# Layer 0's gate and second-norm modulations handed out by the list of stages

## The chip, the cores and the metric

The kernel runs on one core of a Trainium2 chip. The metric is the device time of one execution, in microseconds (us). The engines are TensorE (PE, with its weight loads shown as PEld), VectorE (DVE), ScalarE (ACT), GpSimd (POOL) and SyncE (SP), whose queue issues the DMAs.

## What is computed

A decoder trunk of two layers, over 256 tokens of width 1024, in float32. Cut to what bears on the change:

```python
cond = jax.nn.silu(c)
for l in range(DEPTH):
    mod = cond @ ada_w[l] + ada_b[l]
    sh1, sc1, g1, sh2, sc2, g2 = jnp.split(mod, 6, axis=-1)
    h = rms_norm(x, norm1_g[l]) * (1.0 + sc1) + sh1
    proj = h @ w_in[l]                      # z, xbc, dt, mq, mk, mv, sq, sk, sv
    y = concat(ssd(z, xbc, dt), moba(mq, mk, mv), swa(sq, sk, sv)) @ w_out[l]
    x = x + g1 * y
    h = rms_norm(x, norm2_g[l]) * (1.0 + sc2) + sh2
    x = x + g2 * peer_ffn(h)
```

The six modulations of a layer are vectors of 1024. Here `sh1` and `sc1` are numbers 0 and 1, the gate `g1` is number 2, `sh2` and `sc2` are 3 and 4.

## The kernel before

**One step of a modulation.** A modulation is computed in 8 pieces of 128 channels. One piece is one step: a DMA of 128x1025 floats (512.5 KB, L204, tile `adaw`) and one VectorE instruction that multiplies it by the conditioning row and adds it up into a column of `modc` (L192). `ada_ahead` makes the steps as closures: step i issues the load of piece i+3 and then the VectorE instruction of piece i. In layer 0 the `adaw` tiles are four buffers of the pool `mix0` (tags oH and oL, two each), so a load waits until the instruction on the piece four before it has ended. The same buffers are used at the end of the mixers for the last split of `w_out`.

**Layer 0 has 40 steps before its mixers end.** The first 16 (`early`, modulations 0 and 1) are needed for the first norm: `norm_h` makes `acol` (L264) from them and then h (L284 on VectorE, L282 on ScalarE), two blocks of channels at a time, in four rounds (the loop over `FIRST`). The other 24 (`late`: gate, second shift, second scale) stand in the list `todo`. Their results are read by `gate_row` (L312, the gate) and by the `norm_h` ahead of PEER (modulations 3 and 4), both at the end of the mixers.

**Who takes steps from the list.** `later()` pops steps, two per call (RATE is 2.0). It is called through `tick[0]` each time a chunk of input weights is fetched (in `units`, `proj_parts_whole` and `proj_tokens_whole`), from the stage `rest` on, and four times in the loop over `w_out`. Counted in the code: 8 steps are handed out in `rest` (4 chunks), 2 in `ss`, 4 in `c2`, 4 in `z0`, 4 in `c3` and the last 2 in `z1`.

**Order.** The stages of the mixers follow the string `ORDER[l]`; for layer 0: rest (values and dt), c0 and c1 (convolutions), mv (MoBA's values), ss (sliding-window scores), mp, seg (the decays), c2, z0 (gate z), sv, c3, tok, stb, z1, cb, st, sp. This is the order in which instructions are written down. The kernel is built with `schedule_with_timeline_sim=True`: a planner then chooses the order on each engine by its own estimate of times, and an instruction written earlier goes first among those it takes to be ready. Each engine executes its instructions in the order so chosen. `tc.issue_after(ins)` makes the instructions in its block that are on the engine of `ins` stand behind `ins`.

**dt's chain** is in `values_dt`: L612 adds the bias to dt, L617 to L628 compute softplus on VectorE with two ScalarE activations (L620, L626), and L631 makes `a`, which the decays need (`segr` on GpSimd L642, cumulated sums on TensorE L636, L637, L644).

**Weights.** Projections of the mixers take 512 KB chunks: ScalarE rounds (L173, tile `wH`), and in layer 0 GpSimd makes the remainder in two halves (L176, tile `wL`; `low_of` is "h"). The first projections in layer 0 use the chunks as they are (L360, L375). `wH` and `wL` have three buffers each.

Of the kernel before, what the change touches and what calls it, by code (L numbers as in the profile page):

```python
# [17 lines left out]
ALU = mybir.AluOpType  # L18
# [4 lines left out]
P = 128  # L23
D = 1024
S = 256
NC = 2
# [13 lines left out]
NCAND = 80  # L40
GH = 4
RB = 5
RATE = 2.0
PT = (0, 0)
CV = (1, 0)
WHOLE0 = "mq mk sq xbc0 xbc1"
# [2 lines left out]
    (("- - - mq", "mq"), ("mk mk - sq sq", "mq mk sq"), ("mq - mk -", "mq mk"), ("sq sq", "mq mk sq")),  # L49
)  # L50
ORDER = (
    "rest c0 c1 mv ss mp seg c2 z0 sv c3 tok stb z1 cb st sp",
    "rest c0 mv c1 mp seg ss c2 z0 sv c3 tok stb z1 cb st sp",
)
low_of = ["h"]
# [35 lines left out]
def trunk(ctx: ExitStack, tc: tile.TileContext, x_in, c_in, ada, cols, rows, w_in, w_out, wq, keysT, uT, vT, fg, out, dbg=None):  # L91
    nc = tc.nc
    V, A, G, T = nc.vector, nc.scalar, nc.gpsimd, nc.tensor
# [3 lines left out]
    st = ctx.enter_context(tc.tile_pool(name="st", bufs=2))  # L97
# [218 lines left out]
    tick = [lambda: None]  # L316
# [74 lines left out]
    def mixers(l, xp, mx, xt, xn, modc, colt, early, late):  # L391
        if True:
            def new(shape, tag, dt=F32, bufs=1):
                return mx.tile(shape, dt, tag=tag, name=tag, bufs=bufs)
# [122 lines left out]
                    put_y(self.yn, self.blk0, 2)  # L517

            todo = list(late)
            due = [0.0]  # L520

            def later():
                due[0] += RATE
                while todo and due[0] >= 1.0:
                    due[0] -= 1.0
                    todo.pop(0)()

            xbcT = new([P, 8, S], "xbcT")

# [17 lines left out]
            def gate_z(q):  # L547
                for c, pc in enumerate(proj_tokens(wl, *off[f"z{q}"])):
                    A.activation(sz[c][:, q * 256:(q + 1) * 256], pc[:, :256], AF.Silu)
# [18 lines left out]
            for p, names in enumerate(FIRST[l]):  # L568
# [3 lines left out]
                ada = early[4 * p:4 * p + 4]  # L572
# [10 lines left out]
                        halves.pop(0)()  # L583
            for g in part.values():
                assert next(g, None) is None
            tick[0] = later
            if l == 0:
                proj_tokens_rest = lambda: proj_tokens_whole(wl, *off["rest"], whole)
            else:
# [14 lines left out]
            dt = new([P, NC, 8], "dt")  # L604
            a = new([P, NC, 8], "a")
# [3 lines left out]
            def values_dt():  # L609

                for c, pc in enumerate(proj_tokens_rest()):
                    V.tensor_tensor(out=dtp[:, c, :], in0=pc[:, 0:8], in1=rowt[:, 0:8], op=ALU.add)  # L612
                    A.copy(vx[:, c, :, 0:64], pc[:, 8:392].rearrange("p (h d) -> p h d", d=64))


                na = new([P, NC, 8], "na")
                V.tensor_scalar(out=na, in0=dtp, scalar1=-1.0, scalar2=None, op0=ALU.mult)  # L617
                V.tensor_tensor(out=na, in0=na, in1=dtp, op=ALU.min)
                ey = new([P, NC, 8], "ey")
                A.activation(ey, na, AF.Exp)  # L620
                e1 = new([P, NC, 8], "e1")
                V.tensor_scalar(out=e1, in0=ey, scalar1=1.0, scalar2=None, op0=ALU.add)
                er = new([P, NC, 8], "er")
                V.tensor_scalar(out=er, in0=e1, scalar1=1.0, scalar2=None, op0=ALU.subtract)
                V.tensor_tensor(out=er, in0=ey, in1=er, op=ALU.subtract)
                A.activation(e1, e1, AF.Ln)  # L626
                V.tensor_tensor(out=er, in0=er, in1=e1, op=ALU.add)
                V.scalar_tensor_tensor(out=dt, in0=dtp, scalar=0.0, in1=er, op0=ALU.max, op1=ALU.add)  # L628
                ah = new([P, 8], "ah")
                A.activation(ah, rowt[:, 8:16], AF.Exp)  # L630
                V.scalar_tensor_tensor(out=a, in0=dt, scalar=-1.0, in1=ah[:, None, :].to_broadcast([P, NC, 8]), op0=ALU.mult, op1=ALU.mult)  # L631

            def decays():

# [55 lines left out]
            def swa_scores():  # L690
# [9 lines left out]

            stages = {
                "rest": values_dt, "ss": swa_scores, "mv": moba.values, "mp": moba.put,
                "sv": lambda: att["s"].values(), "sp": lambda: att["s"].put(),
                "c0": lambda: conv(0), "c1": lambda: conv(1), "c2": lambda: conv(2), "c3": lambda: conv(3),
                "z0": lambda: gate_z(0), "z1": lambda: gate_z(1),
                "seg": decays, "tok": tokens, "stb": state_in, "cb": scores_cb, "st": state,
            }
            for name in ORDER[l].split():
                stages[name]()
# [32 lines left out]
            for n in range(2):  # L742
                for q in range(2):
                    h, lo = split(fetch(w_out[l, n, 1, :, q * 1024:(q + 1) * 1024]), LOWM(q))
                    later()
                    for c in range(NC):
                        out_mm(c, n, 1, q, h, lo)
                if n == 0:
                    ssd_out(1)
                put_chunk(n, ysn[n], 4)  # L750
# [294 lines left out]
    for l in range(DEPTH):  # L1045
        own = lambda i: mx.tile([P, D + 1], F32, tag="oL" if i % 2 else "oH", name="adaw", bufs=2)
        adas = ada_ahead([(0, (0, 1), mod[0])] + [(0, (m,), mod[0]) for m in (2, 3, 4)], own, conds[mx]) if l == 0 else []
        h_open(l)
        low_of[0] = "v" if l else "h"
        mixers(l, xp, mx, xt, xn, *mod, adas[:2 * KD], adas[2 * KD:])  # L1050
        if dbg:
            dbg(f"x_mid{l}", xt)
# [108 lines left out]
```

## Time and profile before

| | |
|---|---|
| Time, median of 3 runs | 1942.69 us (1938.9 to 1942.85) |
| The profiled execution's own time | 1945.66 us |
| Its span, first to last instruction | 1943.9 us |
| TensorE busy, share of the span | 1879.8 us, 97% |
| VectorE busy | 1403.6 us, 72% |
| Mean granted TensorE clock | 0.983 |

The mixers of layer 0 fill the first 176 us of the span; there the new x is written out and PEER begins. Times in the rows are us from the start of the span; a bracket at the end of a row of the timeline is how long the engine had been idle and what released it.

### The profile page before, as it was taken

How to read it: one execution, taken by the hardware profiler on the slowest of the kernel's cores; microseconds unless marked ns; L12 is line 12 of the kernel's file. 1: busy time of each engine (PE TensorE's matmuls, PEld its weight loads, DVE VectorE, ACT ScalarE, POOL GpSimd, SP SyncE). 2: the span in 40 equal slices, each digit the busy share in tenths (PEclk: the TensorE clock that was granted, in tenths of full speed). 3: DMA queues.
4: the chain of work that ended last, by engine and by line, in shares of the span. 5: the costliest groups of instructions: out<-in, count | busy, mean ns of one | idle time of the engine just before them, and what ended most of it. 6: DMA issues, size and time to landing. Idle time of an engine off the chain costs nothing. (4 is left out here: it accounts for less than half of the span.)

```text
span 1943.9 us, 33211 instructions
## 1 busy us (share of the span) xinstructions
PE 1879.8 (97%) x12714; PEld 1707.9 (88%) x12714; DVE 1403.6 (72%) x2686; ACT 939.6 (48%) x1473; POOL 420.2 (22%) x255
## 2 busy tenths in 40 slices
PE   7798999999999999999989899999999999999998
PEld 5577999999999888888878789999999998888886
DVE  5955897889963898966657659968899346666665
ACT  2453545544444544545537444455444444555554
POOL 1263789100014001000001147960000320000000
PEclk8889999999999999999999999999999999999999
DMA  9833455444455999865543344554444555665563
GB/s 351 323 126 123 163 167 189 165 158 155 161 165 183 373 357 346 319 205 195 194 129 113 128 148 161 186 184 153 162 154 162 175 184 194 224 196 194 192 194 118
DMA packets 103984, 377.55 MB, mean 194 GB/s; under 512 B 12049, under 2 KB 12305, under 8 KB 103313
## 3 DMA queue, kind: packets, MB, share of 16 engines
q1 hardware_dynamic: 103824, 375.43, 57.1%
q8 instruction: 99, 1.62, 0.4%
q14 instruction: 61, 0.49, 0.1%
HBM read 372.24 MB, written 3.15 MB: 193 GB/s over the span
## 5 line engine op out<-in xcount | busy, mean ns | idle before, releaser
L173 ACT CAST wH<-raw 128x1024 fp32r<-128x1024 f32 x577 | 602.6, 1045 | 517.2 <-PE pu L181 349.1
L176 DVE TENSOR_TENSOR wL<-raw,wH 128x1024 fp32r<-128x1024 f32 (+1 forms) x435 | 532.9, 1226 | 215.7 <-ACT wH L173 214.7
L180 PE MATMUL pu<-hH,wH 128*128 128x256 f32 x2048 | 581.1, 284 | 6.0 <-ACT act L791 6.0
L182 PE MATMUL pu<-hH,wL 128*128 128x256 f32 x2048 | 575.7, 281 | 0.0
L181 PE MATMUL pu<-hL,wH 128*128 128x256 f32 x2048 | 575.3, 281 | 0.0
L176 POOL TENSOR_TENSOR wL<-raw,wH 128x1024 fp32r<-128x1024 f32 (+1 forms) x178 | 365.2, 2071 | 641.0 <-ACT wH L173 620.9
L181 PE MATMUL pacc<-wL,aH 128*128 128x512 f32 x1008 | 393.3, 390 | 0.0
L180 PEld LDWEIGHTS pu<-hH,wH 128*128 128x128 f32 x2048 | 386.4, 189 | 6.8 <-ACT act L791 6.8
L182 PE MATMUL pacc<-wH,aL 128*128 128x512 f32 x1008 | 392.4, 389 | 0.0
L181 PEld LDWEIGHTS pu<-hL,wH 128*128 128x128 f32 x2048 | 386.9, 189 | 0.0
L182 PEld LDWEIGHTS pu<-hH,wL 128*128 128x128 f32 x2048 | 386.6, 189 | 0.0
L180 PE MATMUL pacc<-wH,aH 128*128 128x512 f32 x1008 | 272.5, 389 | 0.0
L999 ACT CAST aH<-act 128x256 fp32r<-128x256 f32 x256 | 103.5, 407 | 323.5 <-PE pacc L181 323.5
L180 PEld LDWEIGHTS pacc<-wH,aH 128*128 128x128 f32 x1008 | 189.3, 188 | 39.5
L182 PEld LDWEIGHTS pacc<-wH,aL 128*128 128x128 f32 x1008 | 189.3, 188 | 39.1
L181 PEld LDWEIGHTS pacc<-wL,aH 128*128 128x128 f32 x1008 | 189.3, 188 | 38.9
L1000 DVE TENSOR_TENSOR aL<-act,aH 128x256 fp32r<-128x256 f32 x256 | 108.2, 425 | 100.1 <-ACT aH L999 99.8
L192 DVE SCALAR_TENSOR_TENSOR adaw<-adaw,crow 128x1025 f32<-128x1025 f32 x96 | 120.5, 1261 | 17.2 <-DMA adaw<-in_ada_dram 17.1
L1089 POOL TENSOR_TENSOR x<-x,fgb 128x512 f32<-128x512 f32 x2 | 2.6, 1293 | 350.0 <-ACT junk L232 350.0
L960 DVE SCALAR_TENSOR_TENSOR act<-pc,act 128x160 f32<-128x160 f32 (+30 forms) x126 | 38.5, 306 | 44.6 <-PE pc L954 44.6
L236 POOL TENSOR_TENSOR hr<-hm,mhalf 128x1 f32<-128x1 f32 x10 | 6.6, 664 | 285.8 <-DVE hm L234 285.8
L946 DVE TENSOR_TENSOR o<-iotax,idx 128x1024 f16<-128x1024 f16 x64 | 47.0, 735 | 17.2 <-ACT idx L915 17.1
(425 smaller groups left out, 2430.9 us busy)
## 6 DMA issues: line engine op xcount, KB each, us to landing
raw<-in_uT_dram SPq DMA_DIRECT2D x256, 512.0 KB, 3.6
raw<-in_vT_dram SPq DMA_DIRECT2D x256, 512.0 KB, 4.4
adaw<-in_ada_dram SPq DMA_DIRECT2D x96, 512.5 KB, 6.0
raw<-in_w_in_dram SPq DMA_DIRECT2D x33, 512.0 KB, 5.4
raw<-in_wq_dram SPq DMA_DIRECT2D x32, 512.0 KB, 3.6
raw<-in_w_out_dram SPq DMA_DIRECT2D x16, 512.0 KB, 3.6
whole<-in_w_in_dram SPq DMA_DIRECT2D x5, 512.0 KB, 10.5
raw<-in_w_in_dram SPq DMA_DIRECT2D x6, 392.0 KB, 3.1
```

The costliest lines, as they stand in the source:

```text
L173: A.copy(h[:, :n], src)
L176: eng.tensor_tensor(out=lo[:, o:o + step], in0=src[:, o:o + step], in1=h[:, o:o + step].bitcast(F32), op=ALU.subtract)
L180: T.matmul(o, l[0], r[0], start=start, stop=False)
L181: T.matmul(o, l[0], r[1], start=False, stop=False)
L182: T.matmul(o, l[1], r[0], start=False, stop=stop)
L192: V.scalar_tensor_tensor(out=src, in0=src, scalar=1.0, in1=cond, op0=ALU.mult, op1=ALU.mult, accum_out=modc[:, m, k:k + 1])
L236: pin[0] = G.tensor_tensor(out=r, in0=ms, in1=mhalf, op=ALU.pow).ins
L946: V.tensor_tensor(out=o1, in0=io, in1=view(idx1), op=ALU.is_equal)
L960: V.scalar_tensor_tensor(out=a, in0=pv[:, lo:hi, :], scalar=1.0 / WSCALE, in1=a, op0=ALU.mult, op1=ALU.mult)
L999: A.copy(aH, act)
L1000: V.tensor_tensor(out=aL, in0=act, in1=aH.bitcast(F32), op=ALU.subtract)
L1089: (V if c else G).tensor_tensor(out=xt[:, c, cs], in0=xt[:, c, cs], in1=fgb[:, cs], op=ALU.mult)
```

## The change

The rate and the tick are gone. `later()` now takes two steps per call and is a stage of its own, `ada`, which stands eight times in layer 0's list, first behind `seg`: 16 steps there, and 8 in the loop over `w_out`, 24 in all as before. All VectorE instructions of these steps are put behind `step`, the instruction at L631 that ends dt's chain. The loads are issued by SP and are not put behind it. In layer 1 the list is empty before and after.

```diff
-RATE = 2.0
 ORDER = (
-    "rest c0 c1 mv ss mp seg c2 z0 sv c3 tok stb z1 cb st sp",
+    "rest c0 c1 mv ss mp seg ada c2 ada ada z0 ada ada sv c3 ada ada tok stb z1 ada cb st sp",
     "rest c0 mv c1 mp seg ss c2 z0 sv c3 tok stb z1 cb st sp",
 )
...
             todo = list(late)
-            due = [0.0]
-
-            def later():
-                due[0] += RATE
-                while todo and due[0] >= 1.0:
-                    due[0] -= 1.0
-                    todo.pop(0)()
+            step_ins = []
+
+            def later(n=2):
+
+                with tc.issue_after(step_ins[0]) if step_ins else nullcontext():
+                    for _ in range(n):
+                        if todo:
+                            todo.pop(0)()
...
             for g in part.values():
                 assert next(g, None) is None
-            tick[0] = later
...
-                V.scalar_tensor_tensor(out=a, in0=dt, scalar=-1.0, in1=ah[:, None, :].to_broadcast([P, NC, 8]), op0=ALU.mult, op1=ALU.mult)
+                step = V.scalar_tensor_tensor(out=a, in0=dt, scalar=-1.0, in1=ah[:, None, :].to_broadcast([P, NC, 8]), op0=ALU.mult, op1=ALU.mult)
+                step_ins.append(step.ins)
...
-                "seg": decays, "tok": tokens, "stb": state_in, "cb": scores_cb, "st": state,
+                "ada": later, "seg": decays, "tok": tokens, "stb": state_in, "cb": scores_cb, "st": state,
```

## Rows read from the trace of the kernel before

**Rows 1.** The page: busy tenths and clock in 40 slices of the span

```profile
PE   7798999999999999999989899999999999999998
PEclk8889999999999999999999999999999999999999
```

**Rows 2.** Stretches: length; busy us of PE, PEld, DVE, ACT, POOL; clock; DMA share; GB/s

```profile
85.20:107.20 22.00, 13.55 (x65) 9.81 (x64) 21.09 (x41) 7.64 (x20) 7.17 (x5) 0.70 0.63 213
107.20:140.00 32.80, 31.79 (x247) 29.82 (x247) 12.83 (x31) 16.55 (x29) 22.92 (x20) 0.99 0.34 113
...
104.00:108.00 4.00, 4.00 (x21) 3.90 (x21) 3.41 (x6) 0.60 (x1) 1.70 (x1) 0.54 0.02 4
```

**Rows 3.** The same for the instructions on adaw alone: busy us of DVE, clock, DMA

```profile
85.20:107.20 22.00, 14.38 (x20) 0.70 0.63 213
```

**Rows 4.** Timeline of VectorE, 47 to 52 us: start, us, line, operation

```profile
47.73 0.16 DVE L264 SCALAR_TENSOR_TENSOR acol<-modc,colt 128x2 f32<-128x2 f32 x1
47.81 1.22 DVE L192 SCALAR_TENSOR_TENSOR adaw<-adaw,crow 128x1025 f32<-128x1025 f32 x1
48.96 1.23 DVE L192 SCALAR_TENSOR_TENSOR adaw<-adaw,crow 128x1025 f32<-128x1025 f32 x1
50.23 1.23 DVE L192 SCALAR_TENSOR_TENSOR adaw<-adaw,crow 128x1025 f32<-128x1025 f32 x1
51.38 0.54 DVE L284 TENSOR_SCALAR h<-pc,acol,modc 128x256 f32<-128x256 f32 x1
```

**Rows 5.** Timeline of TensorE, 30 to 58 us

```profile
30.12 0.70 PE L360 MATMUL pa<-h,raw 128*128 128x256 f32 x2 [0.72 <-DVE h L284]
...
45.76 1.89 PE L360 MATMUL pa<-h,whole 128*128 128x256 f32 x8
47.49 0.60 PE L258 MATMUL pc<-ident,xn 128*128 128x128 f32 x4
51.97 0.70 PE L360 MATMUL pa<-h,whole 128*128 128x256 f32 x2 [3.88 <-DVE h L284]
52.51 0.59 PE L360 MATMUL pa<-h,raw 128*128 128x256 f32 x2
...
53.65 1.06 PE L360 MATMUL pa<-h,raw 128*128 128x256 f32 x2
54.51 2.88 PE L360 MATMUL pa<-h,whole 128*128 128x256 f32 x8
```

**Rows 6.** Timeline of VectorE, 67 to 86 us

```profile
67.41 2.08 DVE L192 SCALAR_TENSOR_TENSOR adaw<-adaw,crow 128x1025 f32<-128x1025 f32 x1
...
74.10 0.16 DVE L486 TENSOR_SCALAR nmm<-mxm 128x8 f32<-128x8 f32 x1
...
85.02 0.18 DVE L631 SCALAR_TENSOR_TENSOR a<-dt,ah 128x16 f32<-128x16 f32 x1
```

**Rows 7.** Timeline of TensorE, 92 to 109 us

```profile
92.77 0.36 PE L636 MATMUL pb<-a,mgt 128*128 128x8 f32 x2 [2.33 <-DVE sc L475]
...
98.27 0.48 PE L420 MATMUL pc<-ident,ynam 128*128 128x128 f32 x1 [4.92 <-DVE yamm L217]
...
98.75 1.92 PE L644 MATMUL pa<-segr,mgt 128*128 128x512 f32 x2
...
102.30 2.07 PE L644 MATMUL pc<-segr,mgt 128*128 128x512 f32 x2 [1.20 <-POOL segr L642]
103.78 0.80 PE L180 MATMUL pc<-hH,wH 128*128 128x256 f32 x1
...
108.58 1.02 PE L644 MATMUL pa<-segr,mgt 128*128 128x512 f32 x2
```

**Rows 8.** Timeline of GpSimd, halves of wL: beside adaw steps, then without

```profile
67.13 5.95 POOL L176 TENSOR_TENSOR wL<-raw,wH 128x512 fp32r<-128x512 f32 x4 [56.30 <-ACT wH L173]
...
112.12 5.03 POOL L176 TENSOR_TENSOR wL<-raw,wH 128x512 fp32r<-128x512 f32 x4 [1.40 <-ACT wH L173]
```

**Rows 9.** Waits of SP's queue, 0 to 180 us: total us, times, longest

```profile
SPq L204 <- DVE adaw L192: 34.2, 22, 5.3
```

## The prediction

> **What bounds the kernel now.** I read the page first: TensorE is busy for nine tenths or more of nearly every slice, at nearly full clock, but not in the first four slices, which are layer 0's mixers [rows 1]. Behind them TensorE is full, so what this stage gains or loses moves the end by as much; the question is only when the mixers of layer 0 end. So I went through that stage by stretches of time, and then through the timelines of TensorE and VectorE side by side, looking for each gap of TensorE and what VectorE did in it.
>
> Three stretches differ. Until about 50 us DMA and the early steps set the pace, and the change leaves both alone. From 51.97 us on TensorE works through the projections; then, between 85.2 and 107.2 us, it is busy 13.55 of 22.0 us at a clock of 0.70, while VectorE is busy 21.09 [rows 2]. Of these 21.09 us, 14.38 are modulation steps [rows 3]: nothing in this stretch needs them. From 107.2 to 140 us it is the other way round: TensorE is busy 31.79 of 32.8 us, VectorE 12.83, and GpSimd 22.92 because it makes the remainders of the weights [rows 2]. So VectorE is the bound of a short early stretch, TensorE that of the rest, and the change takes VectorE work out of the first and puts it into the second.
>
> **Part 1: three late steps ahead of h.** By 47.73 us all 16 early steps are in and `acol` is made. Then three steps of the late list run, and h (L284) begins only at 51.38 us [rows 4]. TensorE waits 3.88 us for it [rows 5]. Its own transposes, which h also needs, had ended at 47.49 + 0.60 = 48.1 us [rows 5], so h could start at about 48.2. With the steps behind L631 they cannot stand there. Gain: 51.38 - 48.2 = 3.2 us. What is late next is the transposes themselves. After the wait the products run slowly: 8 of them take 2.88 us where 8 before it took 1.89, and 2 take 1.06 where 2 take 0.59 [rows 5]; this is the lower of the two clock levels, 1.2 instead of 2.4 GHz, after a gap of 3.88 us. An earlier wait for the same h, of 0.72 us at 30.12, was not followed by this [rows 5]: the 8 products at 45.76 took 1.89. So with a gap of under 1 us the clock should stay: (2.88 - 1.89) + (1.06 - 0.59) = 1.5 us. Part 1 is 4.7 us, and I hold it for the surest term.
>
> **Part 2: steps between 64 and 107 us.** There are 17 of the 24 here; 7 lie before dt's chain ends at 85.02 us [rows 6] and 10 behind it. (Three are those of part 1, and four more ran between 53 and 59 us, where VectorE had nothing else; they lose that free place, which part 3 counts.) The chain of MoBA's maxima, which ends at 74.10, stands behind one that took 2.08 us [rows 6]; and dt's chain, MoBA's values and the sliding-window scores queue among them. In TensorE's order this shows as three waits: 2.33 us for a bank that L475 still reads, 4.92 us for MoBA's normed values, 1.20 us for a decay matrix [rows 7], together 8.45 us. After them the clock is low again: two pairs of L644 take 1.92 and 2.07 us, against 1.02 at 108.58, which costs 1.95 us; and in the stretch from 104 to 108 us, all busy, the clock is 0.54 [rows 2], so 4.0 x (1 - 0.54) = 1.8 us. The most that part 2 can give is 8.45 + 1.95 + 1.8 = 12.2 us: the first product of z0, now at 103.78 us, would follow without waiting, and the first split weights were there at 67.13 + 5.95 = 73.1 us [rows 8].
>
> The least is nothing. The 7 steps ahead of L631 go away, and dt's chain, which now ends at 85.02, should end some 8 us earlier, 4.7 of them from part 1. But the 10 behind it stay behind it, and 14 others join them. What is new for them is the place in the list: they are written behind `seg`, so MoBA's values, the scores and the decays come ahead of them where the planner thinks both are ready; a step that has begun still holds VectorE for 1.22 us. No row shows how the planner will set them. The nearest rows are the two waits of 2.33 and 4.92 us: ahead of both stood steps handed out in earlier stages, which now come later in the list. I take half, 6.1 us, and keep 0 and 12.2 for the range.
>
> **Part 3: 24 steps behind L631.** Here the cost arises. From 85.2 to 140 us VectorE is busy 21.09 + 12.83 = 33.9 us [rows 2], 14.4 of it steps [rows 3], so other work takes 19.5 of 54.8 us and leaves 35.3. If half of part 2 is gained behind L631 this stretch is 3.0 us shorter, 51.8 us with room for 32.3. A step alone takes 1.22 us [rows 4], so 24 take 29.3 and fit. But GpSimd is busy 7.17 + 22.92 = 30.1 of 54.8 us there [rows 2], 55%, and a step beside a GpSimd instruction took 2.08 us [rows 6]; I read four like it, 1.89 to 2.08 us. Taking 2.05 as that price and half of the excess as the mean for a step that starts at a random point: 1.22 + 0.55 x (2.05 - 1.22) / 2 = 1.45 us, or 34.8 for 24, which is 2.5 us more than the room. The 10 steps up to 107.2 us took 14.38 / 10 = 1.44 us each, the reading of the sum included [rows 3]. I take 2.5 us as the cost. Its ends are 0 (all at 1.22) and 24 x 2.05 - 32.3 = 16.9 us (all at 2.05). Behind the steps on VectorE stand the convolutions, the copies of the attention weights and later the scores' mask; TensorE waits for those in its own order.
>
> The rows also show the other side: four halves of `wL` take 5.95 us beside steps and 5.03 without [rows 8]. These halves feed TensorE from 112 us on, one chunk (two halves, 2.5 us) for 24 products. The Trainium skill, on its page "SBUF — State Buffer", section "Who interferes with whom", says that a VectorE instruction with two inputs in SBUF and a GpSimd instruction that reads SBUF share one port, and that the second to come is blocked until the first is through. The trace agrees in direction: 2.08 instead of 1.22 us, and 1.49 instead of 1.26 for a half. The rival called exclusion below works it out from the rows.
>
> **What is moved besides.** Each step issues a DMA on SP's queue, where 22 loads of `adaw` now wait 34.2 us in all for a buffer, 5.3 at most [rows 9], and weight fetches stand behind them. With the list emptied later, the loads of the late steps no longer stand between the chunks of `rest`; they come among those of c2 to z1 and of `w_out`, in a stretch where DMA is busy 0.34 of the time [rows 2]. I cost this at nothing, since five buffers of raw chunks lie ahead of the products; if that cover is gone, a wait of up to 5.3 us is handed on to TensorE. The removed tick itself is no instruction. `gate_row` and the second norm, which read the results, come at the end of the mixers, behind the stretch above.
>
> **The sum.** -3.2 - 1.5 - 6.1 + 2.5 = -8.3 us. The profiled execution took 1945.66 us, 1.8 of it outside its span, and becomes 1937.4. The median of the runs shown is 1942.69, 3.0 us below it; I put the same difference there: **1934.4 us**.
>
> **The rivals.**
> - Full relief: part 2 gives all of 12.2 and the steps fit at 1.22 us. -4.7 - 12.2 = -16.9, or 1925.8 us. For it speaks that all three waits of part 2 have steps ahead of them; against it the GpSimd share.
> - The middle does not move: VectorE is as full behind L631 as before, since 24 steps want to run there instead of 10, and TensorE's order keeps z0 behind the same transposes. -4.7 + 2.5 = -2.2, or 1940.5 us. For it speaks that 14.38 us of steps stood in this stretch already without any pin; against it the new place in the list.
> - Exclusion: steps and GpSimd do not run beside each other at all. Then 29.3 + 30.1 = 59.4 us must fit into 51.8, 7.6 too many, and -10.8 + 7.6 = -3.2 gives 1939.5 us. That a step beside a half takes 2.08 us [rows 6] speaks for some of it; that the four halves beside steps take only 0.9 us more [rows 8] speaks against exclusion from end to end. It is what the rule of the Trainium skill's page "SBUF — State Buffer", section "Who interferes with whom", would give.
> - Slower: every step pays the contended price because GpSimd runs nearly throughout from 112 to 140 us. The 24 steps take 49.2 us, 16.9 more than the room, and push the last convolution, the mask and the gated output, one chain up to 158 us, back by that. -10.8 + 16.9 = +6.1, or 1948.8 us. It decides from a mean price of (32.3 + 10.8 + 3.9) / 24 = 1.96 us for a step. Against it: the mean was 1.44 us in the stretch up to 107.2 us, where GpSimd was busy a third of the time [rows 2, 3].
> - The change does not do what it says: the pin holds only VectorE's instructions. If the planner hoisted them no further than now, part 1 alone would already contradict this, since three steps are certain to leave the place before h. I fold it into the middle that does not move.
>
> **How the numbers follow.** The forecast has a chance of 0.42, with a range of its own from 1930 to 1938.8. Full relief has 0.18, the middle that does not move 0.13, exclusion 0.12, slower 0.15. A measurement of this kernel can tell about 0.2%, 3.9 us, from no change. So faster is 0.42 + 0.18 = 0.60, the same 0.13 + 0.12 = 0.25, slower 0.15. The range reaches down to full relief, 1925, and up past the unchanged cases to 1946, which leaves out most of the slower case and a little below, less than 2 in 10.
>
> **What would show it.** Right: h's last round starts at about 48 us and TensorE's gap there is under 1 us; dt's chain ends near 77 us; z0 starts near 92 to 97 us; x is written out near 168 instead of 176 us. Steps of mean length 1.4 to 1.5 us between 77 and 140 us bear out part 3; 1.8 and more would mean exclusion or worse. Wrong: TensorE gaps released by VectorE, GpSimd's `wL` or late weights after 107 us, of more than 5 us in all; or an order of the planner in which the steps stand in one block ahead of MoBA's values.

## The result

| | before | changed |
|---|---|---|
| Median of five runs each | 1942.69 us (1938.9 to 1947.96) | 1953.48 us (1950.88 to 1955.66) |
| The profiled execution's own time | 1945.66 us | 1953.48 us |
| Its span | 1943.9 us | 1951.8 us |
| Mean granted TensorE clock | 0.983 | 0.983 |

The ratio is 1.0055, with a 95% interval from 1.0035 to 1.0076: the changed kernel is slower, by 10.8 us between the medians. The forecast was 1934.4 us with a range up to 1946. It was wrong in sign, and the time lies outside the range, 4.7 us above the rival called slower.

Up to L631 of the code before, most lines have a number one lower in the changed kernel: L191 is a modulation step, L283 makes h, L630 makes `a`, L175 a remainder of weights. In some experiments they lie a few lines further down.

**Where the time went.** The end of layer 0's mixers is the place to look first, since behind it all kernels of this study need about the same time (1762 to 1768 us from there to the end of the span). The new x is written out at 176.21 us before, and here (timeline of SP, changed kernel):

```profile
186.50 0.33 SPq L1055 DMA_DIRECT2D xd<-x  x1
```

So 10.3 us are lost inside the mixers, and the forecast had expected a gain of some 8 us at this place. (The span is only 7.9 us longer: behind the mixers 2.4 us come back in these two executions, within the 6 us by which that part differs between kernels.) The stretches of [rows 2], and the free stretch ahead of them, for the changed kernel (columns as there: length; busy us of PE, PEld, DVE, ACT, POOL; clock; DMA share; GB/s):

```profile
47.00:64.00 17.00, 16.36 (x78) 12.36 (x78) 6.30 (x15) 7.78 (x15) 4.55 (x4) 1.00 0.73 270
85.20:107.20 22.00, 8.65 (x33) 4.56 (x30) 20.96 (x44) 7.27 (x19) 5.28 (x4) 0.63 0.87 305
107.20:140.00 32.80, 26.92 (x190) 25.73 (x191) 21.04 (x37) 9.98 (x15) 18.24 (x12) 0.88 0.50 175
```

and of the modulation steps alone (busy us of DVE, clock, DMA share, GB/s):

```profile
48.00:190.00 142.00, 34.36 (x48) 0.88 0.52 180
85.20:107.20 22.00, 14.41 (x25) 0.63 0.87 305
107.20:140.00 32.80, 14.65 (x18) 0.88 0.50 175
```

Three things are to be seen. First, VectorE is idle for 10.7 of the 17 us behind the last round of h: nothing takes the place of the steps that stood there. Second, the stretch that the change was to empty holds as much of them as before, 14.41 us against 14.38 [rows 3], and TensorE does 8.65 us of work in it instead of 13.55 [rows 2]. Third, the following stretch has received 14.65 us of steps, and TensorE, full before, is now idle for 5.9 of its 32.8 us; before it was 1.0. The total of the steps, 34.36 us or 1.43 us for each of 24, is almost exactly what the prediction took, 34.8.

**The gaps of TensorE.** Its timeline in the changed kernel; a bracket says how long the engine had been idle and what released it:

```profile
48.71 0.70 PE L359 MATMUL pa<-h,whole 128*128 128x256 f32 x2 [0.64 <-DVE h L283]
...
75.08 0.66 PE L498 MATMUL pa<-vx,pT 128*128 128x65 f32 x2 [4.46 <-DVE na L617]
...
92.16 0.57 PE L636 MATMUL pb<-a,mgt 128*128 128x8 f32 x2 [3.83 <-DVE sc L474]
...
99.62 0.47 PE L419 MATMUL pc<-ident,ynam 128*128 128x128 f32 x1 [6.46 <-DVE yamm L216]
...
104.08 0.47 PE L419 MATMUL pc<-ident,ynam 128*128 128x128 f32 x1 [2.06 <-DVE ynam L442]
...
107.16 0.58 PE L179 MATMUL pc<-hH,wH 128*128 128x256 f32 x1 [0.69 <-ACT wt L646]
...
129.06 0.58 PE L179 MATMUL pb<-hH,wH 128*128 128x256 f32 x1 [5.88 <-ACT sz L549]
...
149.68 0.33 PE L419 MATMUL pb<-ident,ynas 128*128 128x128 f32 x1 [0.78 <-DVE ynas L442]
...
156.75 1.10 PE L721 MATMUL pb<-xdt,wt 128*128 128x64 f32 x8 [1.69 <-POOL wt L680]
...
168.41 0.66 PE L428 MATMUL pa<-ident,yns 128*128 128x128 f32 x4 [2.25 <-DVE ysm L216]
```

The wait for h has shrunk from 3.88 us [rows 5] to 0.64. The three waits of [rows 7], 2.33, 4.92 and 1.20 us, have not gone: the first two are 3.83 and 6.46 us here, another of 2.06 has taken the place of the third, and c2's products begin at 107.16 us instead of 103.78.

These are the products that the prediction and the expectations below call the first of z0. They are c2's: the banks that they write, `pc` and `pa`, are read by its convolution (`conv<-pc`, L542). z0's own, `pa<-wH,hH` in the timeline, follow at 112.32 us before and at 115.76 here. The times stay right, the name does not; below, "c2 starts" stands for it.

Behind that, the kernel before has four waits, too:

```profile
119.98 0.38 PE L180 MATMUL pb<-hH,wH 128*128 128x256 f32 x1 [0.23 <-ACT sz L549]
...
139.33 0.33 PE L420 MATMUL pb<-ident,ynas 128*128 128x128 f32 x1 [0.78 <-DVE ynas L443]
...
146.39 1.10 PE L721 MATMUL pb<-xdt,wt 128*128 128x64 f32 x8 [1.69 <-POOL wt L680]
...
158.12 0.66 PE L429 MATMUL pa<-ident,yns 128*128 128x128 f32 x4 [2.33 <-DVE ysm L217]
```

Three of them are nearly the same in the changed kernel, 0.78, 1.69 and 2.25 us. Only the first has grown, from 0.23 to 5.88 us. It stands ahead of c3's products: they need the bank `pb`, which the activation `sz` of z0's gate must read first. Behind this wait the granted clock is at the lower of its two levels, 1.2 instead of 2.4 GHz, for some 3 us (changed kernel, columns as above):

```profile
129.00:132.00 3.00, 2.94 (x14) 2.94 (x15) 0.00 (x0) 0.94 (x2) 3.00 (x4) 0.51 0.11 26
```

The 20 products behind the wait take 3.75 us (129.06 to 132.81), and took 2.45 before (119.98 to 122.43). So the loss is accounted for: 3.4 us by c2's later start, 5.65 by the longer wait and 1.3 by the clock behind it, together 10.3.

**Why VectorE is late.** Its timeline in the changed kernel, around the end of dt's chain:

```profile
48.11 0.54 DVE L283 TENSOR_SCALAR h<-pc,acol,modc 128x256 f32<-128x256 f32 x1 [0.77 <-PE pc L257]
...
72.58 1.52 DVE L542 SCALAR_TENSOR_TENSOR conv<-pa,colt,conv 128x255 f32<-128x255 f32 x3 [4.27 <-ACT conv L538]
...
79.81 0.18 DVE L630 SCALAR_TENSOR_TENSOR a<-dt,ah 128x16 f32<-128x16 f32 x1
79.90 1.22 DVE L191 SCALAR_TENSOR_TENSOR adaw<-adaw,crow 128x1025 f32<-128x1025 f32 x1
...
81.05 2.06 DVE L191 SCALAR_TENSOR_TENSOR adaw<-adaw,crow 128x1025 f32<-128x1025 f32 x1
...
83.03 1.22 DVE L191 SCALAR_TENSOR_TENSOR adaw<-adaw,crow 128x1025 f32<-128x1025 f32 x1
...
84.18 1.22 DVE L191 SCALAR_TENSOR_TENSOR adaw<-adaw,crow 128x1025 f32<-128x1025 f32 x1
...
85.33 0.55 DVE L497 COPY pT<-pa 128x384 f32<-128x384 f32 x1
```

and the loads of the steps on SP's queue (start, us, line, count):

```profile
47.16 0.33 SPq L203 DMA_DIRECT2D adaw<-in_ada_dram  x1
81.16 3.46 SPq L203 DMA_DIRECT2D adaw<-in_ada_dram  x3
```

The last load was issued at 47.16 us, and the next follows only when the first late step has freed a buffer, at 81.16. So all four buffers had long been loaded when `a` ended, four steps were ready at one stroke, and they stand in a block of 5.4 us directly behind the pin. The copy of MoBA's attention weights (L497) comes behind it, at 85.33 us; before it ran at 85.11, though everything ahead of the block is now 5 us earlier. Without any late step (experiment 1) it comes 2.4 us behind `a`, since it waits for a buffer of `pT`, and here 5.5, so the block holds it for 3.1 us. From 79.90 to 107.5 us 16 steps start; before it was 10 from the end of dt's chain on. Then, ahead of c2's convolution:

```profile
115.16 2.30 DVE L191 SCALAR_TENSOR_TENSOR adaw<-adaw,crow 128x1025 f32<-128x1025 f32 x1
...
117.39 2.31 DVE L191 SCALAR_TENSOR_TENSOR adaw<-adaw,crow 128x1025 f32<-128x1025 f32 x1
...
119.63 2.31 DVE L191 SCALAR_TENSOR_TENSOR adaw<-adaw,crow 128x1025 f32<-128x1025 f32 x1
...
121.87 0.47 DVE L542 SCALAR_TENSOR_TENSOR conv<-pa,colt,conv 128x255 f32<-128x255 f32 x1
122.26 1.90 DVE L191 SCALAR_TENSOR_TENSOR adaw<-adaw,crow 128x1025 f32<-128x1025 f32 x1
...
125.35 0.98 DVE L542 SCALAR_TENSOR_TENSOR conv<-pc,colt,conv 128x254 f32<-128x254 f32 x2
```

Beside them GpSimd makes four halves of `wL` in 7.99 us, where it took 5.03 without steps [rows 8]:

```profile
115.09 7.99 POOL L175 TENSOR_TENSOR wL<-raw,wH 128x512 fp32r<-128x512 f32 x4 [0.94 <-ACT wH L172]
```

The steps start 2.23 and 2.24 us apart, one step and one half in each interval. Alone the two take 1.15 (from 83.03 to 84.18 us, two steps with nothing beside them) and 5.03 / 4 = 1.26 us, together 2.41: here, where both engines have work queued, they run nearly one after the other. The convolution of c2, whose last operation ended at 116.5 us before, ends at 126.3, and only 3.4 us of that are c2's later start. ScalarE waits 7.5 us for it (waits between 70 and 130 us, changed kernel: total, times, longest), and z0's activation `sz` stands behind that on ScalarE; TensorE waits for `sz` at 129.06.

```profile
ACT L543 <- DVE conv L542: 7.5, 1, 7.5
```

### The profile page after: what moved, and what is told of

Read it like the earlier page. It is cut to its first block, busy times and chain, and to the rows that moved or that the text cites. A ratio compares the mean times of both kernels' runs of the same rounds, so it can differ in the third digit from the quotient of the medians.

```text
span 1951.8 us, 33218 instructions
## 1 busy us (share of the span) xinstructions
PE 1878.8 (96%) x12714; PEld 1707.1 (87%) x12714; DVE 1401.2 (72%) x2686; ACT 939.7 (48%) x1473; POOL 425.2 (22%) x255
## 5 line engine op out<-in xcount | busy, mean ns | idle before, releaser
L175 DVE TENSOR_TENSOR wL<-raw,wH 128x1024 fp32r<-128x1024 f32 (+1 forms) x435 | 532.5, 1225 | 215.3 <-ACT wH L172 214.6
L175 POOL TENSOR_TENSOR wL<-raw,wH 128x1024 fp32r<-128x1024 f32 (+1 forms) x178 | 368.1, 2086 | 639.5 <-ACT wH L172 572.7
L191 DVE SCALAR_TENSOR_TENSOR adaw<-adaw,crow 128x1025 f32<-128x1025 f32 x96 | 122.4, 1283 | 19.3 <-DMA adaw<-in_ada_dram 18.9
```

The source lines that it names most:

```text
L175: eng.tensor_tensor(out=lo[:, o:o + step], in0=src[:, o:o + step], in1=h[:, o:o + step].bitcast(F32), op=ALU.subtract)
L191: V.scalar_tensor_tensor(out=src, in0=src, scalar=1.0, in1=cond, op0=ALU.mult, op1=ALU.mult, accum_out=modc[:, m, k:k + 1])
```

## The experiments

The theory after this reading: the pin and the list put the steps at the wrong places, into a block that delays MoBA and into a pack ahead of c2's convolution, while a free place early goes unused. Two rival theories: the port that steps and GpSimd share costs the time; or the changed list has altered TensorE's own order or the fetching of weights, and the steps are innocent. The median of the kernel before in the same series was 1941.80 us (23 runs; first four experiments) and 1941.09 us (29 runs; last four). The bracket behind a ratio is its 95% interval. A time of x written out is that of one profiled execution.

**1. The changed kernel without the late steps.** Left out are the loads and the steps of modulations 2 to 4; their columns are set to 0.5.

```diff
-            todo = list(late)
+            todo = []
+            if l == 0:
+                V.memset(modc[:, 2:5, :], 0.5)
```

> The changed kernel with the 24 late steps of layer 0 left out (their loads too); the columns of the gate, second shift and second scale are set to 0.5 once, so these modulations are not computed. It shows what the steps cost altogether where they now stand. Theory (the steps themselves hold VectorE ahead of work that TensorE waits for): the mixers of layer 0, whose x is written out at 186.5 us in the changed kernel and at 176.2 before, end near 162 us, z0 starts near 90 instead of 107 us, the copy of MoBA's weights right behind dt's chain instead of 5.4 us later, and the time is about 24 us below the changed kernel, 1930 us. Rival (the planner's new order of TensorE, or later weight fetches, is to blame and not the steps): the mixers end at 176 us or later and the time stays above 1942 us.

Measured: 1927.08 us, ratio 0.9921 [0.9897, 0.9946]. c2 starts at 88.75 us, x is written out at 157.79. TensorE in the stretch that was half idle:

```profile
85.20:107.20 22.00, 20.92 (x153) 18.25 (x154) 8.53 (x20) 13.85 (x28) 13.77 (x12) 1.00 0.22 72
```

20.92 of 22 us at full clock, against 8.65 at 0.63 with the steps. List and weights are the same. TensorE's order, which the planner sets anew for each kernel, differs up to c3 only in where the sliding-window scores stand against MoBA's last products, and in a few products of c2, z0 and the decays. So little is left of the third theory: the steps, with their loads, cost 186.50 - 157.79 = 28.7 us at the end of the mixers, out of the 34.4 us that they occupy VectorE. (1.2 of the 28.7 arise ahead of h's last products, which start at 47.48 us here and at 48.71 in the changed kernel. This run does not part steps from loads; experiment 6 keeps both and gains most of it back.) The same figure bounds what a better place can gain with this list: held against it, the steps of the kernel before cost 176.21 - 157.79 = 18.4 us.

**2. Steps with one input in SBUF.** The product with the conditioning row is left out of the late steps; the instruction runs over the same 1025 elements and adds them up. (`mod0` holds layer 0's columns, so that no other step is changed.)

```diff
-        V.scalar_tensor_tensor(out=src, in0=src, scalar=1.0, in1=cond, ...)
+        if m in (2, 3, 4) and modc is mod0[0]:
+            V.tensor_scalar(out=src, in0=src, scalar1=1.0, scalar2=0.0, op0=ALU.mult, op1=ALU.add, accum_out=modc[:, m, k:k + 1])
+        else:
+            V.scalar_tensor_tensor(out=src, in0=src, scalar=1.0, in1=cond, ...)
...
```

> The changed kernel with the VectorE instruction of the 24 late steps replaced by one that reads the weights alone and sums them (the product with the conditioning row is left out); loads, pins and places stay. It tells whether a step costs more beside GpSimd because both read a second operand from SBUF. Theory (sharing between VectorE's second input and GpSimd): the steps between 113 and 124 us, which took 1.9 to 2.3 us in the changed kernel, take 1.2 or less, the four halves of wL that took 7.99 us take about 5.0, c2's convolution comes 4 to 6 us earlier and the time is 5 us lower, about 1948 us. Rival (a step beside a half is slow for another reason, or the mere number of steps counts): steps and halves keep their times and the time stays within 2 us of 1953.5.

Measured: 1948.94 us, ratio 1.0031 [1.0018, 1.0043]; x is written out at 181.70. VectorE, and GpSimd beside it:

```profile
116.08 1.22 DVE L194 TENSOR_SCALAR_CACHE_REDUCE adaw<-adaw 128x1025 f32<-128x1025 f32 x1
...
117.37 1.22 DVE L194 TENSOR_SCALAR_CACHE_REDUCE adaw<-adaw 128x1025 f32<-128x1025 f32 x1
```

```profile
112.84 5.03 POOL L175 TENSOR_TENSOR wL<-raw,wH 128x512 fp32r<-128x512 f32 x4 [1.39 <-ACT wH L172]
```

The lengthening is gone on both engines, 1.22 and 1.26 us again, with both at work at the same time. So it goes with the form that has two inputs in SBUF, and not with both being busy. The Trainium skill, on its page "SBUF — State Buffer", section "Who interferes with whom", says that a VectorE instruction with two inputs in SBUF and a GpSimd instruction that reads SBUF exclude each other, and that one with at most one such input, outside the two-port modes, does not contend; both halves of that agree with these rows. But it is worth 4.8 us at the end of the mixers (4.5 in the medians), of the 28.7 that the steps cost; the other 24 they cost at their plain length, by their place. TensorE's wait ahead of c3 shows it: it is still there, and 4.59 us long.

```profile
125.52 0.46 PE L179 MATMUL pb<-hH,wH 128*128 128x256 f32 x1 [4.59 <-ACT sz L554]
```

**3. The steps of the list behind c2's last convolution.** The two steps handed out ahead of it stay where they are.

```diff
+            last_conv = [None]
...
-                        V.scalar_tensor_tensor(out=acc[:, s:], in0=pc[:, :S - s], ...)
+                        last_conv[0] = V.scalar_tensor_tensor(out=acc[:, s:], in0=pc[:, :S - s], ...)
...
+                if q == 2:
+                    step_ins[:] = [last_conv[0].ins]
```

> The changed kernel, but from the second place in the list on (22 of 24 steps) the steps are pinned behind the last convolution instruction of c2 instead of the end of dt's chain. Theory (the steps between 80 and 124 us cost three times: four of them ahead of the copies of MoBA's weights, about 5 us; those up to 107 us ahead of the normed values, about 3; those beside the halves of wL ahead of c2's convolution, about 7): z0 starts near 95 us, c2's convolution ends within 2 us of its products, and the mixers end between 168 and 176 us, since the steps now stand beside the halves of c3 and z1 where VectorE is half empty; about 1940 us. Rival (any 22 steps behind dt's chain overfill VectorE beside GpSimd, wherever they are pinned): the wait moves to the copies of the sliding window or to c3 and the mixers end at 183 us or later, above 1950 us.

Measured: 1953.99 us, ratio 1.0052 [1.0036, 1.0069]; x is written out at 188.11. The theory's numbers were missed, and the rival's came in: 183 us or later, above 1950. VectorE:

```profile
106.90 0.48 DVE L543 SCALAR_TENSOR_TENSOR conv<-pc,colt,conv 128x253 f32<-128x253 f32 x1
...
151.00 2.29 DVE L191 SCALAR_TENSOR_TENSOR adaw<-adaw,crow 128x1025 f32<-128x1025 f32 x1
...
162.34 0.68 DVE L726 TENSOR_TENSOR yz<-pb,xsd 128x512 f32<-128x512 f32 x1
```

and TensorE behind it:

```profile
168.71 1.12 PE L428 MATMUL pa<-ident,yns 128*128 128x128 f32 x4 [6.59 <-DVE ysm L216]
```

The first half went as the theory has it: c2 starts at 94.49 us, its convolution ends at 107.4, 19 us earlier than in the changed kernel. Then the steps come out on the other side: TensorE waits 2.36 us for a copy of attention weights (at 116.35) and 5.20 us for the sliding window's normed values (at 135.59). Six more steps, five of them at about 2.3 us, stand between 148.78 and 162.34 us ahead of the gated output, for which TensorE waits 6.59 us. The mean step took 42.38 / 24 = 1.77 us. There is no room late; 22 steps moved there arrive on the next chains.

**4. The kernel before, with its late steps behind h.** `done[0]` is the last round of h; list, rate and tick are those of before.

```diff
-                    todo.pop(0)()
+                    with tc.issue_after(done[0]):
+                        todo.pop(0)()
```

> The kernel before with one pin: the late steps stand behind the last VectorE instruction that makes h. This is part 1 of the prediction alone. In the changed kernel h came at 48.1 instead of 51.4 us and the products of rest ended at 70.0 instead of 74.9 us, so part 1 was right as far as it went. Theory (the gain of part 1 is kept where no steps are bunched behind dt's chain): rest ends near 70 us, the mixers end near 171 to 172 us, and the time is 4 to 5 us below the kernel before, 1938 us. Rival (the queue of VectorE between 64 and 107 us takes the gain back whatever stands ahead of it): rest ends near 70 us, but z0 starts at 103 to 104 us as before, and the time is within 1 us of 1942.7.

Measured: 1937.60 us, ratio 0.9976 [0.9964, 0.9989]: 4.2 us faster than before. This is part 1 of the prediction alone, and it is near what that part said, 4.7 us. (In its trace x is written out 6.7 us earlier, at 169.48.)

**5. The changed kernel without the pin.**

```diff
-                with tc.issue_after(step_ins[0]) if step_ins else nullcontext():
+                with nullcontext():
```

> The changed kernel without the pin: the list of stages gives the steps out, and the planner may set them as early as it likes. Only the pin behind dt's chain is undone. Theory (the pin is to blame: it takes the idle time of VectorE between 50 and 64 us away from the steps and leaves 24 of them for the time behind 80 us): three steps stand ahead of h again, so h comes near 51.4 us, but all steps are through before c2's convolution, the mixers end between 172 and 178 us, and the time is 1940 to 1945 us. Rival (the list's late places are to blame, whatever pins the steps): the mixers end above 182 us and the time stays above 1949 us.

Measured: 1946.63 us, ratio 1.0025 [1.0016, 1.0035]; x is written out at 180.57. Both lie between what theory and rival expected. So the new list is no better than the tick of before by itself, and slightly worse. The steps ran early again, three ahead of h (TensorE waits 3.97 us), and dt's chain ended only at 90.79 us. Three steps, from 75.70, 77.62 and 78.76 us on, stand ahead of the first operation on dt's second bank, and two more, from 86.32 and 87.55, inside the chain; what else delays it was not followed further.

**6. The changed kernel with the pin behind h instead of `a`.**

```diff
-                with tc.issue_after(step_ins[0]) if step_ins else nullcontext():
+                with tc.issue_after(done[0]):
```

> The changed kernel with the steps pinned behind the last VectorE instruction of h instead of the end of dt's chain; the list stays. Against the kernel before with the same pin (1937.6 us, x written out at 169.5) only the list differs from the tick. Theory (the point of the pin decides, not the list): five or more steps run in VectorE's idle time right behind h, none is left behind c2's convolution, x is written out at 168 to 172 us, and the time is 1936 to 1940 us. Rival (the list costs by itself): 1943 us or more.

Measured: 1933.43 us, ratio 0.9947 [0.9927, 0.9967], the fastest kernel here that computes everything: 7.7 us faster than before, and 2.6 us below what was expected of it (four runs, one of them at 1927.27). c2 starts at 96.60 us, x is written out at 164.84. Between the two TensorE waits only twice, and not for `sz`:

```profile
145.00 0.50 PE L180 MATMUL pc<-wL,yH 128*128 128x512 f32 x1 [0.72 <-POOL wL L175]
...
146.76 0.66 PE L428 MATMUL pa<-ident,yns 128*128 128x128 f32 x4 [1.03 <-DVE ysm L216]
```

Its stretches:

```profile
47.00:64.00 17.00, 16.36 (x79) 12.36 (x78) 14.39 (x28) 6.50 (x13) 2.50 (x2) 1.00 1.02 395
85.20:107.20 22.00, 18.88 (x108) 14.84 (x108) 21.68 (x44) 11.69 (x27) 7.90 (x9) 0.84 0.57 190
107.20:140.00 32.80, 32.80 (x255) 31.50 (x254) 20.35 (x34) 18.77 (x31) 25.84 (x21) 1.00 0.43 145
```

In the first stretch VectorE is busy 14.39 us instead of 6.30, and TensorE does the same 16.36 us of work as with the late pin: the steps of this stretch cost it nothing there. Fourteen steps run ahead of `a`, though `a` itself ends only at 83.89 us, and the last step of all ends at 104.5, before the convolution of c2. From 107.2 to 140 us TensorE is full.

**7. The changed kernel with the pin behind the sliding window's maxima** (the instruction that negates them in `Attend.scores`), at about 90 us.

```diff
+                    neg = V.tensor_scalar(out=nm, in0=m, scalar1=-1.0, scalar2=None, op0=ALU.mult)
+                    if self.sink is not None:
+                        step_ins[:] = [neg.ins]
...
-                step_ins.append(step.ins)
+                if not step_ins:
+                    step_ins.append(step.ins)
```

> The changed kernel with the pin moved further down, behind the sliding window's negated maxima, so that no step stands between dt's chain and MoBA's normed values. All 24 steps are left for the time after that. Theory (what costs is where the steps stand: ahead of the normed values, and later beside GpSimd): z0 starts near 95 us instead of 107, seven steps run in the idle time of VectorE before c2's convolution, some ten stand behind it beside GpSimd and up to the gated output at 1.7 us or more in the mean, and the mixers end between 176 and 184 us, 1943 to 1951 us. Rival (only the block of four steps behind dt's chain costs): the mixers end below 172 us, under 1939 us.

Measured: 1944.44 us, ratio 1.0013 [1.0003, 1.0023]; x is written out at 177.17. c2 starts at 89.46 us, nearly as early as without any step (88.75) and 14.3 us earlier than before, and all of that and more is lost later; the longest wait of TensorE is one of 7.26 us for the sliding window's normed values (at 134.58). GpSimd at the pin:

```profile
95.95 17.06 POOL L175 TENSOR_TENSOR wL<-raw,wH 128x512 fp32r<-128x512 f32 x8 [0.71 <-ACT wH L172]
```

Eight halves at 2.13 us each instead of 1.26: here the steps of 2.30 us also hold up the weights, and TensorE waits 1.15 and 1.24 us for them (at 106.43 and 108.64).

**8. Two places: eight steps behind h, sixteen behind the maxima.** Experiment 7, and besides:

```diff
+            def early_tick():
+                with tc.issue_after(done[0]):
+                    for _ in range(2):
+                        if todo:
+                            todo.pop(0)()
+
+            tick[0] = early_tick
...
+            def rest_stage():
+                values_dt()
+                tick[0] = lambda: None
...
-                "rest": values_dt, "ss": swa_scores, ...
+                "rest": rest_stage, "ss": swa_scores, ...
```

> Eight late steps are given out while the weights of rest are fetched, pinned behind h; the other 16 by the list, pinned behind the sliding window's negated maxima. So none stands between about 66 us and the end of MoBA's and the window's scores, and few beside the halves of wL. Theory: the first eight run in VectorE's idle time and cost nothing, z0 starts near 95 us, the convolution of c2 comes 2 to 5 us behind its products because a few steps stand ahead of it, and x is written out at 164 to 168 us, which makes 1932 to 1936 us, the fastest with all steps in. Rival (16 steps behind 90 us overfill VectorE beside GpSimd as 24 did): c2's convolution waits 8 us or more, the mixers end at 174 us or later, and the time is 1941 us or more.

Measured: 1938.54 us, ratio 0.9982 [0.9972, 0.9991]; x is written out at 173.88. The theory's 1932 to 1936 us were missed: the time is better than before, but worse than experiment 6 by 5.1 us, and x comes about when the rival said. The sixteen late ones reach the weights and the convolution again; VectorE and TensorE:

```profile
108.16 2.31 DVE L191 SCALAR_TENSOR_TENSOR adaw<-adaw,crow 128x1025 f32<-128x1025 f32 x1
...
115.24 0.46 DVE L544 SCALAR_TENSOR_TENSOR conv<-pc,colt,conv 128x253 f32<-128x253 f32 x1
```

```profile
116.53 0.58 PE L179 MATMUL pb<-hH,wH 128*128 128x256 f32 x1 [4.70 <-ACT sz L551]
```

**Together.** Time, and where x is written out, ordered by where the pin stands (the 24 steps are the same in all but the first). The medians come from three series, in which the kernel before took 1942.69, 1941.80 and 1941.09 us, so differences of 1 or 2 us between rows say nothing:

| steps | median us | x written out, us | mean us of one step |
|---|---|---|---|
| left out | 1927.08 | 157.79 | |
| before: tick, no pin | 1942.69 | 176.21 | 1.34 |
| list of the change, no pin | 1946.63 | 180.57 | 1.30 |
| tick of before, behind h (about 48 us) | 1937.60 | 169.48 | |
| list of the change, behind h | 1933.43 | 164.84 | 1.33 |
| 8 behind h, 16 behind the maxima | 1938.54 | 173.88 | 1.47 |
| the change: behind `a` (80 us) | 1953.48 | 186.50 | 1.43 |
| behind the maxima (90 us) | 1944.44 | 177.17 | 1.64 |
| behind c2's convolution (107 us) | 1953.99 | 188.11 | 1.77 |

The list alone moves the end of the mixers by +4.4 us without a pin and by -4.6 with the pin behind h; the point of the pin, at the same list, moves it by -15.7 (h), +5.9 (`a`) and -3.4 (the maxima) against no pin.

## Why the prediction was wrong, step by step

The sum by parts, where x is written out (forecast, then measured): part 1 -4.7 and -4.9 us, part 2 -6.1 and +8.3, part 3 +2.5 and +6.9, together -8.3 and +10.3. The measured ones are read as follows: the products of rest end at 69.96 us instead of 74.90; c2 starts 3.4 us later all the same, which makes 8.3 for part 2; the wait for `sz` and the clock behind it are part 3.

**Part 1 was right.** h starts at 48.11 us (said: 48.2), the gap is 0.64 us (under 1), the clock stays: the 17 us from 47 are granted at 1.00. Experiment 4 has this part alone and gives 4.2 us for the 4.7 said.

**Part 2 failed, and with it the sum.** Half of 12.2 us was to be gained; instead c2 starts 3.4 us later. Two steps of its working are at fault. The first was "dt's chain, which now ends at 85.02, should end some 8 us earlier, 4.7 of them from part 1". It ended 5.2 us earlier: the shift of part 1 and hardly more. Taking away the seven steps ahead of it gained nothing, since another wait took their place: on VectorE dt stands behind a convolution of c1, which waits 4.27 us for ScalarE (at 72.58). Without any late step the chain still ends only at 77.99 us, with the same wait of 4.26 us in it, and TensorE's wait ahead of the attention's products is still there with 3.88 us. The second was that the new place in the list lets "MoBA's values, the scores and the decays come ahead of them where the planner thinks both are ready". That looks at the list and not at what is ready at the pin: the loads are not pinned, so four steps are ready at 79.90 us, while the copies and scores come one by one. The prediction named this sign among the wrong ones, one block ahead of MoBA's values, but gave it no time. Since 16 steps instead of 10 start up to 107.5 us, TensorE's waits between `a` and c2 are 13.8 us in all instead of the 8.45 of [rows 7]. That is 5.4 us of the 8.3; another 1.7 are longer waits ahead of `a`, and the rest, some 1.3, goes with a lower clock (0.63 instead of 0.70). The prediction had only asked whether VectorE is relieved before `a`; behind `a` the stretch kept 14.41 us of steps. The rival called the middle that does not move had said just that, but took for granted that part 1 would be kept. (That the list can help is shown behind another pin: with both pins behind h, experiments 6 and 4, it is worth 4.6 us.)

**Part 3 had the price right and the cost wrong.** The mean was to be 1.45 us and was 1.43. What failed is the step from price to time: "leaves 35.3" us of room, and so only an excess over the room costs anything. Room summed over 55 us says nothing of an in-order queue. Steps packed into 113 to 124 us hold the convolution behind them, by 6.5 us beyond c2's later start, though VectorE is idle elsewhere (7.37 us ahead of 134.63), and TensorE waits 5.88 us for what follows. The prediction's sign for this, more than 5 us of gaps behind 107 us released by VectorE, GpSimd or weights, did not fit: this wait is released by ScalarE, which stands behind VectorE's convolution, and the other gaps are in the kernel before too. The rival called slower named a queue of VectorE's behind the steps (the last convolution, the mask, the gated output) but tied it to a mean price of 1.96 us. c2's convolution was held at a mean of 1.43 (1.90 to 2.31 in the pack alone), and 4.59 us of TensorE's wait stay with all steps at 1.22 (experiment 2), while the waits for mask and gated output did not grow. So the rival had the right queue, the wrong condition and the wrong place in it; its chance of 0.15 came from that condition. That the measured time lies near its 1948.8 us is chance: 8.3 us of the loss are part 2's.

**The free place was undervalued.** That four steps "lose that free place, which part 3 counts" was half a sentence. The stretch from 47 to 64 us takes six steps at 1.22 us without costing TensorE anything there (experiment 6), and the late pin closes it. This is the largest difference between the kernels: the same list with the pin 32 us earlier writes x out 21.7 us earlier. Of these, c2's start is 107.16 - 96.60 = 10.6, and the waits of TensorE behind it are 10.6 us in the changed kernel and 1.75 in experiment 6, 8.85 less; of the last 2.2 us, 1.3 are the low clock behind the wait for `sz`.

**Exclusion** was set aside because four halves took only 0.9 us more. That row has steps beside a part of the halves only. Where both queues are full the exclusion is nearly complete, as the intervals of 2.23 us show, but it costs 4.5 us here and does not decide the sign: without it (experiment 2) the kernel is still slower than before.

**The loads** were costed at nothing. SP now waits 41.1 us for buffers up to 180 us, against 34.2 [rows 9], and no gap of TensorE is released by a raw chunk. But three late steps wait for their own loads, 2.1 us in all. One of them, 0.81 us at 101.75, stands right ahead of MoBA's normed values (L442 at 102.90), for which TensorE waits 2.06 us. So the term was not quite nothing, though under 1 us as far as the trace shows.

What stays open is the rest of the delay of dt's chain in experiment 5.

## What to carry to other kernels

Work moved to a stretch with "room" cost here by what stands behind it on its in-order engine, not by the sum of what is free: list the consumers behind the new place one by one, and ask what is ready at the first moment of the pin, loads that run ahead included. In this kernel filler work belongs into the earliest stretch in which its engine is idle and nothing on the path needs that engine; pin it behind the last instruction that it must not delay (here h), not behind a later one. And leave the filler out once: that run shows about how much a better placement can still gain (0.79% here, of which the best one got 0.53%).

## What the runs showed of the hardware

A VectorE instruction with two inputs in SBUF (`scalar_tensor_tensor` with an accumulated output, 128x1025) and GpSimd's `tensor_tensor` (128x512) exclude each other nearly completely where both have work queued: 2.23 us from step to step with one half of `wL` in between, against 1.15 and 1.26 us alone, 2.41 one after the other. The accumulating form with one input, over the same 1025 elements, runs at 1.22 us beside GpSimd and leaves its halves at 1.26 (experiment 2).
